# Four value blocks in the lead, and the outputs of a recurrence group made behind its chain

## The chip, the cores and the metric

The kernel runs on one core of one Trainium2 chip. The metric is the device time of one execution in microseconds (us), lower is better. Of several executions the median is compared; one more execution was profiled, and all views come from that one.

## The reference, cut to what matters

A trunk of two layers over 256 tokens and 2048 channels, in float32. Layer 0 mixes tokens with an RWKV-7 recurrence, layer 1 with differential attention; each is followed by a gated MLP. Only layer 0's mixer is touched:

```python
def rwkv7_mix(x, v_first, vres, mu, w_rkv, ...):
    xx = token_shift(x) - x                       # x of the token before, less x
    xr, xw, xk, xv, xa, xg = (x + xx * mu[i] for i in range(6))
    r, k, v = xr @ w_rkv[0], xk @ w_rkv[1], xv @ w_rkv[2]
    w = -softplus(-(w0 + tanh(xw @ w1) @ w2)) - 0.5          # low-rank: decay
    a = sigmoid(a0 + (xa @ a1) @ a2)                         # low-rank
    g = sigmoid(xg @ g1) @ g2                                # low-rank
    ...
    # 32 heads of 64: S_t = S_{t-1} (diag(w_t) + a_t^T b_t) + v_t^T k_t ;  y_t = S_t r_t
    y = wkv7_scan(r_h, decay, k_h, v_h, -kk, kk * a_h)
    ...
    return (group_norm(y) + bonus) * g @ w_o
```

## The kernel before

Everything is kept transposed: a tile holds 128 channels (one *block*) by 256 tokens, and there are 16 blocks of the 2048 channels (`KT`). Products in full float32 precision are made of three faster ones: `split` and `chunk` cut a number into a rounded part `hi` (a ScalarE cast) and the rest `lo` (a subtraction on VectorE, `L219` for weights and `L197` for inputs), and hi*hi, hi*lo and lo*hi are summed in PSUM. An input tile holds its hi and lo parts side by side, 512 columns. `mm3` makes the three products either as one of 512 columns and one of 256 (`L231`, `L232`) or, when `narrow`, as three of 256 in one half bank (`L227`, `L228`, `L229`). Weights come from memory in chunks of four k-blocks (256 KB, `L210`), into the pools `raw`, `hi` and `lo`, whose buffer counts `PACE["vw"]` sets for this stage.

The work is written as Python generators; each `yield` ends a step, and `_together` interleaves several generators by the share of their steps. A scheduler of the framework then orders each engine's queue, and may move an instruction past others of its engine. Queues run in order.

Layer 0 has these stages. In the *lead*, `lead` feeds `mix(3, ...)`, which loads the input blocks (`L775`), makes `xx` and the mixed input of the value product into the tile `S0`, and beside it runs the products of the first value blocks (`lg` of them), going through the k-blocks in step with the input. For the first `ramp` k-blocks the products of the two blocks alternate (`L251` to `L255`). Then `_together` runs the rest of the value products in pairs (`dense_pair`) beside `loras`, which mixes three more inputs into the tile `S1` (the chip's rows say `S1r`) and makes the three low-rank products. Then the r and k products of the first group follow, beside the mix for k.

Then comes the recurrence, in eight groups of two blocks (four heads). `pipeline` runs at once the `chain` and `outputs` of a group, the `lanes` of the next one, the `front` of the one behind it and the r and k products of the one behind that. `lanes` inverts 64x64 triangles in small products (`L1254` to `L1302`). `chain` goes through the four chunks of 64 tokens: it finishes R (`L1369`), copies it, makes U (`L1381`) and copies it, and makes the next state S (`L1392`, `L1396`). The outputs y of a chunk (PSUM tile `yps`) are two kinds of products: of the state (`L1373`), written just behind `L1369`, and of U and V (`L1402`), written just behind `L1392`. `outputs` normalizes y of the group. Single PSUM tiles `us`, `b0`, `b1`, `yps` serve all groups.

Of the kernel before, what the change touches and what calls it, by code (L numbers as in the profile page):

```python
# [36 lines left out]
            4), lb=1, early=46.23, vw=(8, 5, 5), vp=2, ep='V', eg='A', lg=2, lr=2, la=4, ah=10, ao=12, ah0=0.05)  # L37
# [92 lines left out]
class Trunk:  # L130
# [103 lines left out]
    def dense_steps(self, src, n, xs, evac, group=1, k0=0, step=4, pool=False, narrow=False,  # L234
                    ramp=0):

        for g in range(0, len(src), group):
# [4 lines left out]
            while done < n:  # L242
                if done < ramp:

                    chunks = [(ps[j], *next(its[j])) for j in js]
                    s = chunks[0][2]
                    for i in range(s):
                        x = xs[:, k0 + done + i, :]
                        w = slice(i * P, (i + 1) * P)
                        for p, _, _, hi, lo in chunks:  # L250
                            self.nc.tensor.matmul(p[:, :T], lhsT=hi[:, w], rhs=x[:, :T], start=done + i == 0,  # L251
                                                  stop=False)
                            self.nc.tensor.matmul(p[:, T:], lhsT=lo[:, w], rhs=x[:, :T], start=False, stop=False)
                        for p, _, _, hi, lo in chunks:
                            self.nc.tensor.matmul(p[:, T:], lhsT=hi[:, w], rhs=x[:, T:], start=False, stop=False)  # L255
                        yield
                    done += s
                    continue
# [248 lines left out]
    def lead(self, feed, group, *args, ramp=0, ahead=4):  # L507
# [246 lines left out]
    def rwkv(self, ahead=None):  # L754
        nc, tc = self.nc, self.tc
        with ExitStack() as ctx:
# [5 lines left out]
            with ExitStack() as c1:  # L762
                gr = Groups(self, c1, S1, V, mids)
                with ExitStack() as c2:
# [6 lines left out]
                    xx = xp.tile([P, KT, T], F32, name="xx")  # L771
                    nc.gpsimd.memset(x[:, :, 0:1], 0.0)
# [6 lines left out]
                    def mix(i, dst, first=False):  # L779
                        for j in range(KT):  # L780
                            if first and j in starts:
                                load(j, starts.get(j))
# [723 lines left out]
```

## Time and profile before

| | |
|---|---|
| median of three runs | 2523.8 us (2520.84 to 2527.0) |
| the profiled execution | 2523.33 us |
| its span in the trace | 2521.6 us |
| TensorE busy (PE) | 2457.5 us, 97% |
| VectorE busy (DVE) | 2012.7 us, 80% |
| ScalarE busy (ACT) | 1640.7 us, 65% |
| GpSimd busy (POOL) | 165.7 us, 7% |
| DMA | 428.70 MB, mean 170 GB/s |
| mean granted TensorE clock | 0.991 |

The profile names engines PE (TensorE's products), PEld (its weight loads), DVE, ACT, POOL and SP (the queue that issues the DMAs). A row of a timeline has the start, the duration, engine, line, operation, output<-input, shape and count, and in brackets the idle time before it with what ended it. A row of the waits has who waited for whom, the sum, the times, and the longest. A row of a group has the count, busy time, mean duration in ns, and the idle time before. By time, the lead lasts until 33.8 us, the stage with it until 154 us, the recurrence until about 617 us.

### The profile page before, as it was taken

How to read it: one execution, taken by the hardware profiler on the slowest of the kernel's cores; microseconds unless marked ns; L12 is line 12 of the kernel's file. 1: busy time of each engine (PE TensorE's matmuls, PEld its weight loads, DVE VectorE, ACT ScalarE, POOL GpSimd, SP SyncE). 2: the span in 40 equal slices, each digit the busy share in tenths (PEclk: the TensorE clock that was granted, in tenths of full speed). 3: DMA queues.
4: the chain of work that ended last, by engine and by line, in shares of the span. 5: the costliest groups of instructions: out<-in, count | busy, mean ns of one | idle time of the engine just before them, and what ended most of it. 6: DMA issues, size and time to landing. Idle time of an engine off the chain costs nothing.

```text
span 2521.6 us, 56316 instructions
## 1 busy us (share of the span) xinstructions
PE 2457.5 (97%) x18626; PEld 2166.4 (86%) x18626; DVE 2012.7 (80%) x5097; ACT 1640.7 (65%) x4237; POOL 165.7 (7%) x232
## 2 busy tenths in 40 slices
PE   7999999999999999999999999999999999999997
PEld 6997888777888888888889899988988888888886
DVE  8978888878997777776776877779987777777776
ACT  5756666545676666665666766666776666666665
POOL 1000000000300000000110200003300000000111
PEclk9999999999999999999999999999999999999998
DMA  6644443344465555666766555556465555566664
GB/s 211 199 127 108 111 107 103 106 126 126 142 200 189 190 190 190 189 190 198 215 188 188 151 167 175 169 178 184 152 200 188 188 187 189 187 188 187 189 189 139
DMA packets 276742, 428.70 MB, mean 170 GB/s; under 512 B 60632, under 2 KB 83168, under 8 KB 276448
## 3 DMA queue, kind: packets, MB, share of 16 engines
q1 hardware_dynamic: 276448, 425.10, 55.7%
q8 instruction: 146, 2.39, 0.4%
q14 instruction: 148, 1.21, 0.2%
HBM read 420.25 MB, written 6.31 MB: 169 GB/s over the span
## 4 chain that ended last, share of the span: by engine, by line
PE 81%; DVE 4%; ACT 1%; issue 1%; DMA 1%; POOL 0%; ACTq 0%; DVEq 0%; POOLq 0%
PE psd L231 43%; PE psd L232 22%; PE psd L227 2%; PE psd L228 2%; PE psd L229 2%; DVE lo L219 1%; PE psd L298 1%; PE psd L299 1%; PE psd L297 1%; DMA raw<-in_ff_up 1%; PE pss L1168 1%; PE lnst L353 0%; DVE S L197 0%; ACT hi L216 0%; PE pss L675 0%
## 5 line engine op out<-in xcount | busy, mean ns | idle before, releaser
L216 ACT CAST hi<-raw 128x256 fp32r<-128x256 f32 (+1 forms) x3036 | 1219.2, 410 | 690.5 <-PE psd L231 464.5
L219 DVE TENSOR_TENSOR lo<-raw,hi 128x256 fp32r<-128x256 f32 (+1 forms) x3034 | 1303.0, 439 | 417.2 <-ACT hi L216 373.4
L231 PE MATMUL psd<-S,hi 128*128 128x512 f32 x3000 | 1054.5, 395 | 2.6 <-DVE S L197 1.4
L232 PE MATMUL psd<-S,lo 128*128 128x256 f32 x3000 | 841.1, 280 | 3.0 <-DVE lo L219 3.0
L231 PEld LDWEIGHTS psd<-S,hi 128*128 128x128 f32 x3000 | 565.0, 188 | 133.8 <-ACT hi L216 1.7
L232 PEld LDWEIGHTS psd<-S,lo 128*128 128x128 f32 x3000 | 564.6, 188 | 5.0 <-DVE lo L219 4.7
L231 PE MATMUL psd<-hs,hi 128*128 128x512 f32 x1290 | 451.2, 394 | 0.0
L232 PE MATMUL psd<-hs,lo 128*128 128x256 f32 x1290 | 361.5, 280 | 0.0
L231 PEld LDWEIGHTS psd<-hs,hi 128*128 128x128 f32 x1290 | 241.8, 187 | 56.2 <-ACT hi L216 0.6
L232 PEld LDWEIGHTS psd<-hs,lo 128*128 128x128 f32 x1290 | 243.1, 188 | 0.3 <-DVE lo L219 0.2
L227 PE MATMUL psd<-S,hi 128*128 128x256 f32 x480 | 138.9, 289 | 2.2 <-ACT hi L216 1.9
L229 PE MATMUL psd<-S,lo 128*128 128x256 f32 x480 | 138.6, 289 | 0.7 <-DVE lo L219 0.7
L228 PE MATMUL psd<-S,hi 128*128 128x256 f32 x480 | 137.9, 287 | 0.0
L231 PE MATMUL psd<-S1r,hi 128*128 128x512 f32 x276 | 108.9, 425 | 2.3 <-ACT hi L216 1.1
L227 PEld LDWEIGHTS psd<-S,hi 128*128 128x128 f32 x480 | 90.8, 189 | 6.7 <-ACT hi L216 2.6
L229 PEld LDWEIGHTS psd<-S,lo 128*128 128x128 f32 x480 | 90.7, 189 | 5.7 <-issue 3.0
L228 PEld LDWEIGHTS psd<-S,hi 128*128 128x128 f32 x480 | 91.0, 190 | 2.0 <-issue 1.7
L227 PE MATMUL psd<-S1r,hi 128*128 128x256 f32 x284 | 85.7, 302 | 0.1
L231 PE MATMUL psd<-S1a,hi 128*128 128x512 f32 x240 | 84.6, 396 | 0.0
L371 POOL COPY ln_acc<-X 128x256 f32<-128x256 f32 x4 | 2.0, 511 | 1242.6 <-DVE X L405 1242.6
L232 PE MATMUL psd<-S1r,lo 128*128 128x256 f32 x276 | 82.0, 297 | 1.4 <-DVE lo L219 1.4
L546 DVE SCALAR_TENSOR_TENSOR gc<-gp,cpar,gc 128x256 f32<-128x256 f32 x172 | 82.2, 478 | 0.0
(304 smaller groups left out, 3541.6 us busy)
## 6 DMA issues: line engine op xcount, KB each, us to landing
raw<-in_ff_up SPq DMA_DIRECT2D x676, 256.0 KB, 3.4
raw<-in_ff_down SPq DMA_DIRECT2D x320, 256.0 KB, 2.9
raw<-in_rkv SPq DMA_DIRECT2D x192, 256.0 KB, 3.7
raw<-in_da_qk SPq DMA_DIRECT2D x122, 256.0 KB, 3.4
raw<-in_da_v SPq DMA_DIRECT2D x64, 256.0 KB, 3.0
raw<-in_da_o SPq DMA_DIRECT2D x64, 256.0 KB, 3.7
raw<-in_rw_o SPq DMA_DIRECT2D x50, 256.0 KB, 3.4
raw<-in_ff_down SPq DMA_DIRECT2D x32, 192.0 KB, 2.6
```

The source lines that it names most:

```text
L216: nc.scalar.copy(out=hi[:, :s * P], in_=r)
L219: eng.tensor_tensor(out=lo[:, :s * P], in0=r, in1=hi[:, :s * P].bitcast(F32), op=ALU.subtract)
L227: nc.tensor.matmul(ps[:, :T], lhsT=hi, rhs=xs[:, :T], start=first, stop=False)
L228: nc.tensor.matmul(ps[:, :T], lhsT=hi, rhs=xs[:, T:], start=False, stop=False)
L229: nc.tensor.matmul(ps[:, :T], lhsT=lo, rhs=xs[:, :T], start=False, stop=last)
L231: nc.tensor.matmul(ps, lhsT=hi, rhs=xs, start=first, stop=False)
L232: nc.tensor.matmul(ps[:, T:], lhsT=lo, rhs=xs[:, :T], start=False, stop=last)
L297: nc.tensor.matmul(o, lhsT=xh, rhs=hi, start=k == 0 and b == 0, stop=False)
L298: nc.tensor.matmul(o, lhsT=xh, rhs=lo, start=False, stop=False)
L299: nc.tensor.matmul(o, lhsT=xl, rhs=hi, start=False, stop=k == KT - 1 and b == T // P - 1)
L546: nc.vector.scalar_tensor_tensor(out=gc, in0=g[:, k:k + T], scalar=cw(k, j), in1=gc, op0=ALU.mult, op1=ALU.add)
L1168: nc.tensor.matmul(ps[:, n * P:(n + 1) * P], lhsT=KB[hr, uu, :, :], rhs=AR[hr, uu, :, :], start=True, stop=True)
```

## The change

Two edits. In the lead, four value blocks instead of two go through the k-blocks with the input, each with its own PSUM bank and in narrow form; there is no `ramp`, and the lo parts of the lead's first chunks are made on VectorE, not on GpSimd. The mixed input of the lead is made without `xx`, as (1 - mu) x_t, scaled on ScalarE (`L777`), plus mu x_(t-1) on VectorE (`L778`). `xx` is made later, in four operations of 1024 columns on VectorE, ahead of the first low-rank mix; in all later mixes two blocks are split at once, 512 columns wide. The pools hold 9 raw, 8 hi and 8 lo chunks instead of 8, 5 and 5, and PSUM has six banks here instead of four. The four value blocks are evacuated by one ScalarE copy each.

In the recurrence, all y products of a group are written behind its fourth chunk, for which all states of the group are kept (six state tiles instead of two). `chain` and `lanes` have one more step each.

```diff
-            4), lb=1, early=46.23, vw=(8, 5, 5), vp=2, ep='V', eg='A', lg=2, lr=2, la=4, ah=10, ao=12, ah0=0.05)
+            4), lb=1, early=46.23, vw=(9, 8, 8), vp=4, ep='V', eg='A', lg=4, la=4, ah=10, ao=12, ah0=0.05)
@@ dense_steps
-                if done < ramp:
...
 def lead
-                steps = self.dense_steps(*args, group=group, pool=True, ramp=ramp)
+                steps = self.dense_steps(*args, group=group, narrow=True)
@@ rwkv
-                    def mix(i, dst, first=False):
-                        for j in range(KT):
...
-                                eng = nc.vector if j in (0, 4, 8, 12) else nc.gpsimd
-                                eng.tensor_tensor(out=xx[:, j, :], in0=x[:, j, 0:T], in1=x[:, j, 1:],
-                                                  op=ALU.subtract)
...
+                    def mix(i, dst, first=False, diff=False):
+                        for j in range(0, KT, 1 if first else 2):
...
+                                nc.scalar.activation(out=t, in_=x[:, j, 1:], func=AF.Copy, scale=om[:, j:j + 1])
+                                nc.vector.scalar_tensor_tensor(out=m, in0=x[:, j, 0:T], scalar=self.p(f"mu{i}", j),
+                                                               in1=t, op0=ALU.mult, op1=ALU.add)
+                                self.split(m, dst[:, j, :])
...
+                            if diff and j % 4 == 0:
+                                self.tc.keep_in_program_order(
+                                    nc.vector.tensor_tensor(out=xx[:, j:j + 4, :], in0=x[:, j:j + 4, 0:T],
+                                                            in1=x[:, j:j + 4, 1:], op=ALU.subtract))
...
+                            self.split(m, dst[:, j:j + 2, :])
...
-                    evv = lambda j, ps: self.total(ps, V[:, j, :])
+                    evv = lambda j, ps: nc.scalar.copy(out=V[:, j, :], in_=ps[:, :T])
...
-                                       for j in range(n, KT, 2))), 13 * 5))
+                                       for j in range(n, KT, 2))), 11 * 5))
@@ Groups.open
-        self.Ss = [fx.tile([P, GT, C], F32, name=f"S{i}") for i in range(2)]
+        self.Ss = [fx.tile([P, GT, C], F32, name=f"S{i}") for i in range(2 * (NC - 1))]
@@ lanes
         nc.vector.tensor_copy(out=Z2[rows[3]], in_=pv[rows[3]])
         yield
+        yield
@@ chain
-                for jj in range(GT):
-                    for h in range(2):
-                        nc.tensor.matmul(yps[rows[h], jj, cs], lhsT=S[rows[h], jj, :],
-                                         rhs=AR[rows[h], jj * NC + c, 1, :], start=jj == 0, stop=False)
...
+            S = Sn
+            yield
+
+        for c in range(NC):
+            cs = slice(c * C, (c + 1) * C)
+            if c:
+                for jj in range(GT):
+                    for h in range(2):
+                        nc.tensor.matmul(yps[rows[h], jj, cs], lhsT=states[c - 1][rows[h], jj, :],
+                                         rhs=AR[rows[h], jj * NC + c, 1, :], start=jj == 0, stop=False)
             for jj in range(GT):
                 for h in range(2):
                     nc.tensor.matmul(yps[rows[h], jj, cs], lhsT=UV[:, jj, c, h, :], rhs=m(jj, h, c)[:, C:],
                                      start=c == 0 and jj == 0, stop=jj == GT - 1)
-            S = Sn
-            yield
+        yield
```

What the scheduler makes of it, at three places. A row is one instruction, or several equal ones that follow each other. First VectorE's queue in the middle of the lead, before: `mx` is the mixed input, `xz` the input, `S_76` the tile `S0`.

```order
L792 SCALAR_TENSOR_TENSOR mx<-xx,par,xz 128x256 x3
L197 TENSOR_TENSOR S_76<-mx,S_76 128x256 x2
L792 SCALAR_TENSOR_TENSOR mx<-xx,par,xz 128x256
L197 TENSOR_TENSOR S_76<-mx,S_76 128x256
L219 TENSOR_TENSOR lo<-raw,hi 128x512
L197 TENSOR_TENSOR S_76<-mx,S_76 128x256
L789 TENSOR_TENSOR xx<-xz 128x256
L219 TENSOR_TENSOR lo<-raw,hi 128x512
```

And the same queue in the changed kernel (`mp` is the mixed input now):

```order
L778 SCALAR_TENSOR_TENSOR mp<-xz,par,mp 128x256
L219 TENSOR_TENSOR lo<-raw,hi 128x512
L778 SCALAR_TENSOR_TENSOR mp<-xz,par,mp 128x256
L197 TENSOR_TENSOR S_76<-mp,S_76 128x256
L219 TENSOR_TENSOR lo<-raw,hi 128x512
L197 TENSOR_TENSOR S_76<-mp,S_76 128x256
```

In the lead one lo part of weights now stands between any two input blocks; sixteen are in it instead of six, and the differences `xx` have gone behind it.

Second, TensorE in group 3 around R of chunk 1, before (`S_2191` is the state behind chunk 0, `psd` rows are dense products of another group):

```order
L1392 MATMUL us<-UV,KBT 64x64 x4
L1402 MATMUL yps<-M,UV 64x64 x4
L1227 MATMUL pss<-cst,KB 128x128 x4
L227 MATMUL psd<-S_76,hi 128x256
L1369 MATMUL b_5972<-S_2191,AR 64x64
L1369 MATMUL b_5973<-S_2191,AR 64x64
L1369 MATMUL b_5972<-S_2191,AR 64x64
L1369 MATMUL b_5973<-S_2191,AR 64x64
L1373 MATMUL yps<-AR,S_2191 64x64 x4
L228 MATMUL psd<-S_76,hi 128x256
```

After it ten more dense products come, and then `L1381`, which needs R. In the changed kernel (`L1389` is the old `L1392`, `L1377` the old `L1381`, `L1409` and `L1405` the two kinds of y products):

```order
L1389 MATMUL us<-UV,KBT 64x64 x4
L1227 MATMUL pss<-cst,KB 128x128 x4
L227 MATMUL psd<-S_76,hi 128x256
L228 MATMUL psd<-S_76,hi 128x256
L1409 MATMUL yps<-M,UV 64x64
L1369 MATMUL b_5884<-S_2101,AR 64x64
L1369 MATMUL b_5885<-S_2101,AR 64x64
L1369 MATMUL b_5884<-S_2101,AR 64x64
L1369 MATMUL b_5885<-S_2101,AR 64x64
L1409 MATMUL yps<-M,UV 64x64 x3
L1405 MATMUL yps<-AR,S_2101 64x64 x3
L1377 MATMUL us<-R,M 64x64 x4
```

The y products were written behind the whole chain, but the scheduler has drawn some of them forward into the chain as soon as their inputs exist. Between the state products and the use of R only six of them are left. Of the 28 of such a group, ten stand in one run behind the last U.

Third, ScalarE in the same group, where the copy of the lanes' last intermediate (`L1295`) stands; before:

```order
L1075 COPY M<-W_5075 32x8x32 x2
L844 CAST l_5872<-l2r 128x256
L1320 ACT_TABLE_LOAD
L1320 ACTIVATE wa<-psd,par 128x256
L1295 COPY T_5828<-pss 32x256
L1320 ACTIVATE wa<-psd,par 128x256
L1075 COPY UV<-us 64x2x2x128 x2
```

and in the changed kernel:

```order
L309 ACTIVATE o_rs<-Lx 128x512
L1295 COPY T_5740<-pss 32x256
L844 CAST l_5761<-l2r 128x256
L1075 COPY M<-W_4987 32x8x32
L1321 ACT_TABLE_LOAD
L1321 ACTIVATE wa<-psd,par 128x256
L1309 COPY M<-pss 32x8x32
L1321 ACTIVATE wa<-psd,par 128x256
L1075 COPY UV<-us 64x2x2x128
```

The copy has moved ahead of the table load, with the additional step of the lanes; the second copy of `UV` has moved behind the sigmoids.

More of the change, by code (lines that the diff above doesn't have):

```diff
@@ L232, in mm3, with dense_steps @@
             nc.tensor.matmul(ps[:, T:], lhsT=lo, rhs=xs[:, :T], start=False, stop=last)
-    def dense_steps(self, src, n, xs, evac, group=1, k0=0, step=4, pool=False, narrow=False,
-                    ramp=0):
+    def dense_steps(self, src, n, xs, evac, group=1, k0=0, step=4, pool=False, narrow=False):
         for g in range(0, len(src), group):
@@ L242, in dense_steps @@
             while done < n:
-                if done < ramp:
[L245 to L255, printed above, removed]
-                        yield
-                    done += s
-                    continue
                 for j in js:
@@ L505, in ln_finish, with lead @@
             nc.sync.dma_start(out=out[:, j:j + 2, :], in_=xs)
-    def lead(self, feed, group, *args, ramp=0, ahead=4):
+    def lead(self, feed, group, *args, ahead=4):
         fed = 0
@@ L777, in rwkv @@
                     starts = {0: 1, 1: 2, 2: 4, 4: 6, 6: 8, 8: 10, 10: 12, 12: 14, 14: 16}
[L779 to L794 removed]
+                    def mix(i, dst, first=False, diff=False):
+                        for j in range(0, KT, 1 if first else 2):
+                            if first:
+                                if j in starts:
+                                    load(j, starts.get(j))
+                                if j == 0:
+                                    nc.sync.dma_start(out=self.par[:, :6 * KT], in_=self.a["par"][:, :6 * KT])
+                                    nc.scalar.activation(out=om, in_=self.p(f"mu{i}", 0, KT), func=AF.Copy, scale=-1.0,
+                                                         bias=1.0)
+                                if j == 8:
+                                    self.load_consts()
+                                m = xt.tile([P, 2, T], F32, name="mp")
+                                t, m = m[:, 0], m[:, 1]
+                                nc.scalar.activation(out=t, in_=x[:, j, 1:], func=AF.Copy, scale=om[:, j:j + 1])
[3 more added lines that the diff above has]
+                                yield
+                                continue
+                            if diff and j % 4 == 0:
+                                self.tc.keep_in_program_order(
+                                    nc.vector.tensor_tensor(out=xx[:, j:j + 4, :], in0=x[:, j:j + 4, 0:T],
+                                                            in1=x[:, j:j + 4, 1:], op=ALU.subtract))
+                            m = xt.tile([P, 2, T], F32, name="mp")
+                            for k in range(2):
+                                nc.vector.scalar_tensor_tensor(out=m[:, k], in0=xx[:, j + k, :],
+                                                               scalar=self.p(f"mu{i}", j + k), in1=x[:, j + k, 1:],
+                                                               op0=ALU.mult, op1=ALU.add)
+                                if k == 0:
+                                    yield
+                            self.split(m, dst[:, j:j + 2, :])
@@ L798, in loras @@
                         for i, mi, fn in ((0, 1, AF.Tanh), (1, 4, None), (2, 5, AF.Sigmoid)):
-                            yield from mix(mi, S1)
+                            yield from mix(mi, S1, diff=i == 0)
                             def ev(_, ps, i=i, fn=fn):
@@ L814, in rwkv @@
                     self.lead(mix(3, self.S0, True), n, [rkv[2][j] for j in range(n)], KT, self.S0, evv,
-                              ramp=PACE["lr"], ahead=PACE["la"])
+                              ahead=PACE["la"])
                     _together((loras(), 4 * 16 + 3 * 5),
```

18 lines of the change are left out of this document (6 added, 12 removed).

## The prediction

> **What bounds the kernel now.** I read the page's engine shares first, then who TensorE waits for in the first stage, then the busy time by stage.
>
> ```profile
> span 2521.6 us, 56316 instructions
> PE 2457.5 (97%) x18626; PEld 2166.4 (86%) x18626; DVE 2012.7 (80%) x5097; ACT 1640.7 (65%) x4237; POOL 165.7 (7%) x232
> PE psd L251 <- ACT hi L216: 8.8, 2, 8.0
> PE psd L232 <- DVE lo L219: 2.5, 1, 2.5
> 8.00:26.50 18.50, 11.47 (x37) 8.90 (x38) 16.18 (x31) 8.63 (x22) 9.59 (x11) 0.82 0.65 224
> 33.80:154.00 120.20, 119.50 (x959) 116.72 (x958) 112.04 (x253) 82.40 (x175) 3.94 (x15) 1.00 0.59 182
> 277.00:469.00 192.00, 186.41 (x3029) 160.43 (x3028) 167.71 (x437) 125.08 (x301) 2.78 (x12) 1.00 0.40 106
> ```
>
> TensorE is busy 97% of the span, so time is won only where it stands still, runs at half clock, or repeats work. The two waits are the longest of the first 33.8 us; in the stage rows the columns after the length are TensorE, weight loads, VectorE, ScalarE, GpSimd, then granted clock, DMA share and GB/s. From 33.8 to 154 TensorE has no hole, but VectorE is nearly as full (112 of 120). The profiled run took 2523.3 us, 1.7 more than its span, and 0.5 below the median 2523.8; the sum is made against 2523.3. Everything behind layer 0's recurrences stands in the same order before and after, so only the first 617 us count.
>
> **The lead: TensorE's side.**
>
> ```profile
> 7.36 0.62 ACT L216 CAST hi<-raw 128x512 fp32r<-128x512 f32 x1 [2.95 <-DMA raw<-in_rkv]
> 22.98 0.58 PE L232 MATMUL psd<-S,lo 128*128 128x256 f32 x1 [2.45 <-DVE lo L219]
> 24.00 0.63 PE L231 MATMUL psd<-S,hi 128*128 128x512 f32 x1
> 24.64 0.63 PE L231 MATMUL psd<-S,hi 128*128 128x512 f32 x1
> 26.95 0.39 PE L231 MATMUL psd<-S,hi 128*128 128x512 f32 x1
> 27.30 0.39 PE L231 MATMUL psd<-S,hi 128*128 128x512 f32 x1
> 33.83 0.28 PE L229 MATMUL psd<-S,lo 128*128 128x256 f32 x1
> 154.14 0.29 PE L227 MATMUL psd<-mid,l 128*128 128x256 f32 x1
> ```
>
> A 512- and a 256-column product take 0.64 us at 24.0 (half clock) and 0.35 at 26.95 (full): 0.213 or 0.117 us per 256 columns. The three narrow products of the new code are the same 768 columns, so the change of form costs nothing. Two blocks are 2 x 16 x 3 x 0.117 = 11.2 us of work, yet their last product is issued just before 33.83: about 22 us are lost. The first cast ends at 8.0 and waited for its transfer; the new queue has the same transfers ahead of that one, so 8.0 stays. The first lo part, now on VectorE, is ready 0.7 later, at 8.7. One step (a chunk of four k for one block) is 12 narrow products: 2.56 us at half clock. VectorE and ScalarE supply one in about 1.4 us (below), so TensorE has no more holes, and its clock should open as it did before: 4.0 us after the dense run that starts at 22.98 the spacing is short. So 19 products run until 12.7, and the other 173 take 20.2: the lead ends near 33.0, with four blocks instead of two. The rest of the stage, to 154.14, shrinks by the 0.8 us and by 96 products (11.3): TensorE alone would end it at 142.0, a gain of 12.1.
>
> **The lead: VectorE's side.**
>
> ```profile
> L792 DVE SCALAR_TENSOR_TENSOR mx<-xx,par,xz 128x256 f32<-128x256 f32 x6 | 5.3, 940 | 0.0
> L197 DVE TENSOR_TENSOR S<-mx,S 128x256 fp32r<-128x256 f32 x5 | 3.5, 745 | 0.0
> L219 DVE TENSOR_TENSOR lo<-raw,hi 128x512 fp32r<-128x512 f32 x44 | 29.4, 679 | 0.0
> L792 DVE SCALAR_TENSOR_TENSOR mx<-xx,par,xz 128x256 f32<-128x256 f32 x44 | 19.6, 473 | 0.0
> L197 DVE TENSOR_TENSOR S1r<-mx,S1r 128x256 fp32r<-128x256 f32 x41 | 15.7, 411 | 0.1
> L216 ACT CAST hi<-raw 128x512 fp32r<-128x512 f32 x42 | 26.1, 620 | 10.8 <-PE psd L228 4.9 <-ACT hi L216 2.3 <-PE psd L231 2.1
> L196 ACT CAST S1r<-mx 128x256 fp32r<-128x256 f32 x41 | 16.1, 407 | 5.7 <-DVE mx L792 5.5
> 24.13 1.26 DVE L792 SCALAR_TENSOR_TENSOR mx<-xx,par,xz 128x256 f32<-128x256 f32 x3
> 26.31 1.10 DVE L197 TENSOR_TENSOR S<-mx,S 128x256 fp32r<-128x256 f32 x3 [0.92 <-ACT S L196]
> 29.03 1.89 DVE L219 TENSOR_TENSOR lo<-raw,hi 128x512 fp32r<-128x512 f32 x3
> 30.00:142.00 112.00, 111.30 (x879) 108.05 (x879) 110.30 (x253) 83.34 (x181) 0.00 (x0) 1.00 0.63 195
> ```
>
> The first two rows are of 9 to 18 us, the next five of 40 to 100. While GpSimd made differences and lo parts beside it, VectorE's multiply-add took 940 ns instead of 473 and its split 745 instead of 411. The change takes all fourteen GpSimd operations of the lead away, so I count the quiet durations; were the slow ones to stay, 29 such operations would cost about 12 us more, which I exclude because nothing is left on GpSimd there. Back to back they overlap: three in a row take 1.26, 1.10 and 1.89, so each beyond the first adds 0.39, 0.345 and 0.60 us.
>
> From the first lo part (8.0) the lead needs 16 lo (9.6), 12 multiply-adds (4.7) and 13 splits (4.5): 18.8 us, to 26.8. ScalarE's share is as long: 12 steps of a cast (0.62), an input cast and the new scaled copy (no row shows it; I take 0.41 like the input cast, as the operand is as wide), 1.37 with overlap, and 4 casts, 18.9. They hand to each other, so I add 1.2 for such stalls: 28.0. Bounds: 26.8, and 32 if each of 12 steps lost 0.4.
>
> Behind it VectorE must make, until the last lo of the first r products, 68 lo (48 value, 12 low-rank, 8 r; 40.8 us), 80 multiply-adds (31.2), 40 splits now two blocks wide (24.0 at the lo's 0.60, the same 512 columns), 4 differences of 1024 columns (no row; stretching 411 and 679 gives 1.22, less overlap 1.15; 4.6) and 9 small ones (3.1): 103.7, to 131.7. The totals of the whole stage hardly change: the wide splits save 40 x (0.69 - 0.60) = 3.6 and the two evacuations 0.7, the differences and the two lo parts that GpSimd had cost 5.8. TensorE would want that last lo at 129.2 (142.0 less 11.4 for the k products and 1.4 for one chunk). VectorE is 2.5 late; with 0.5 of latency TensorE is held to 145.0. The old code had 110.3 of 112 us here, so the stage was as much VectorE's as TensorE's, and deeper weight buffers (8 instead of 5) create no capacity. I take another 1.1 for short waits on the way: 146.1, **a gain of 8.0 us**. The ends are 12.1 (no lag) and 4 (VectorE at 32).
>
> The transfers: 16 chunks (4.2 MB), the inputs (2.1), parameters and constants (0.3), 6.6 MB, go ahead of the last step.
>
> ```profile
> 0.00:10.00 10.00, 1.21 (x4) 0.92 (x4) 1.95 (x5) 2.92 (x4) 3.98 (x10) 1.00 0.72 206
> 10.00:20.00 10.00, 6.22 (x24) 4.92 (x23) 10.00 (x16) 3.90 (x10) 7.72 (x10) 0.99 0.84 296
> ```
>
> With 2.1 MB in the first 10 us (206 GB/s) and 296 GB/s from then on they are in at 25.2, and the last step's cast and lo part end at 26.5, beside VectorE's 26.8: the cover is there, but thin; a quarter slower behind 10 us would cost 5, which the end of 32 holds. The four evacuations become one ScalarE copy each, behind casts, with six banks free: nothing.
>
> **The recurrence.** The number of y products is the same. Their order is not one run: in groups 1 to 4 it is cut into pieces.
>
> ```profile
> PE pss L1302 <- ACT T L1295: 0.8, 1, 0.8
> PE pss L1263 <- DVE M L1171: 0.3, 1, 0.3
> PE pss L1123 <- DVE bon L1191: 0.3, 1, 0.3
> 374.06 1.28 ACT L1320 ACT_TABLE_LOAD   x1
> 375.85 0.36 ACT L1295 COPY T<-pss 32x256 f32<-32x256 f32 x1
> 371.03 0.28 PE L228 MATMUL psd<-S1r,hi 128*128 128x256 f32 x1
> 371.15 0.28 PE L229 MATMUL psd<-S1r,lo 128*128 128x256 f32 x1
> 371.36 0.73 PE L1282 MATMUL pss<-W,Z 32*32 32x16 f32 x64
> PE us L1392 <- DVE UV L1075: 0.8, 1, 0.8
> PE b L1369 <- DVE S L1396: 0.8, 1, 0.8
> 229.01 0.69 PE L1293 MATMUL pss<-T,M 32*32 32x32 f32 x32 [0.98 <-DVE T L1287]
> 230.00:240.00 10.00, 9.37 (x66) 6.87 (x65) 6.71 (x20) 6.85 (x16) 0.00 (x0) 0.66 0.15 36
> ```
>
> The three waits are all of group 2 (325 to 373 us). For: the copy L1295 now stands ahead of the table load on ScalarE, so the 0.8 goes, in five groups 4. There are 14 fewer runs of small products in all; entering one costs 0.09 (0.21 against 0.12 in the rows of 371) and leaving it 0.03, so 1.7. Against: between the state product and the use of R stood 11 narrow products, now six tiny ones; both copies of R need a semaphore and about 0.2 us, so 0.3 once per group. L1168 comes ahead of VectorE's last AR operation (about 0.6), L1263 loses four products of cover (0.5), and L1123 waits for a VectorE chain that is no shorter. That is 1.4 in four groups, 5.6. Net 0.1; I take **-0.5**. Ends: 6 of gain; and 6 of loss, if each of eight groups takes the 0.8 us of a bare hand-over, as the rows at L1392 and L1369 show it in the last groups. The extra step in the lanes queues nothing new; the order shows what waits behind it.
>
> The sum: 2523.3 - 8.0 - 0.5 = 2514.8, said as 2515.
>
> **Rivals.** (a) VectorE, late in the lead, eats most of the gain: 32 instead of 28 leaves 4, and the chain gives back 1: 2520. For it: 110.3 of 112; against: GpSimd no longer slows it. (b) All goes well: no VectorE lag (12.1), the chain's 6 and no half clock: 2505 or less. (c) Slower, through the clock in the recurrence. In the row at 230 the granted clock is 0.66, just after a wait of 1.0 us amid tiny products: 6.8 of the 10 us ran at half clock, which costs 3.4. If the new waits (1.4 per group) do the same, with 1.0 for themselves beyond what goes, it is 4.4 in each of six groups, 26, less the lead's 8, and the time is 2541; from 2.2 us per group on it is measurably slower. Against: group 2 has 1.3 us of waits and a granted clock of 1.00. [...] (d) The lead's clock stays half: 192 x 0.213 puts its end at 49.6 instead of 33.0, past the 45.1 where it breaks even, and the time at 2528; only holes would do that, and supply is faster than TensorE's 2.56.
>
> **Numbers.** Forecast 55% (2509 to 2519), (a) 22%, (b) 14%, (c) 6%, (d) 3%. The range goes from (b)'s edge into (a) and a little beyond: 2505 to 2524. A measurement tells 0.2%, 5 us, from no change: faster 0.72 (forecast and (b), with a little of (a)), same 0.21, slower 0.07.
>
> **What would show it.** Right: the fourth block's last lead product near 33, the half clock gone by 13 to 16 us, VectorE without 0.9-us multiply-adds, TensorE waiting for lo (L219) between 40 and 130 us by some 3 us in all, and the low-rank products that follow the k products near 146. L1303 without its 0.8; small new waits at L1377, L1168 and L1263. Wrong: a wait for hi or a transfer inside the lead, VectorE done with it later than 30, or half-clock windows in groups 1 to 4.

## The result, and the profile after

The changed kernel takes 2511.57 us (median of four runs, 2508.72 to 2513.36) beside 2523.57 for the kernel before in the same session: a ratio of 0.9948, 95% interval 0.9934 to 0.9963, or 12 us less. The same kernel, timed again on another occasion (below), gave 2511.32 and a ratio of 0.9959 (0.9946 to 0.9971). The forecast was 2515, within 2505 to 2524. The profiled execution took 2512.88 us, 10.4 less than the one of before. First two lines of the page, then the busy time by stage, where the columns after the length are TensorE, weight loads, VectorE, ScalarE, GpSimd, clock, DMA share and GB/s.

```profile
span 2510.9 us, 56277 instructions
PE 2461.2 (98%) x18650; PEld 2170.1 (86%) x18650; DVE 2009.3 (80%) x5057; ACT 1635.2 (65%) x4215; POOL 154.5 (6%) x218
```

```profile
13.00:33.00 20.00, 20.00 (x171) 20.00 (x171) 20.00 (x43) 18.19 (x44) 0.00 (x0) 1.00 0.94 312
33.00:145.80 112.80, 109.20 (x867) 105.87 (x866) 105.60 (x204) 70.73 (x129) 4.64 (x15) 1.00 0.57 175
268.70:459.70 191.00, 190.88 (x3027) 164.07 (x3026) 168.07 (x434) 122.28 (x302) 1.88 (x12) 1.00 0.41 106
459.70:629.20 169.50, 160.97 (x1862) 123.61 (x1861) 135.66 (x365) 90.67 (x234) 6.94 (x13) 0.98 0.41 119
```

From 13 to 33 us TensorE and VectorE have no hole now and GpSimd does nothing; behind it TensorE stands still for 3.6 of 112.8 us. In the four steady groups (268.7 to 459.7) TensorE is busy 190.9 of 191.0 us, where it was busy 186.4 of 192.0: nearly all waits are gone, and yet the stretch is hardly shorter. The row of before for the last groups and the way to the next stage:

```profile
468.70:638.20 169.50, 158.41 (x1863) 123.28 (x1862) 136.01 (x364) 90.78 (x233) 6.97 (x13) 0.96 0.41 119
```

It has the same 169.5 us, though a granted clock of 0.96 there stands for 13.7 us at half clock, and the 0.98 after for 6.8. Next, rows of TensorE's and VectorE's timelines of the changed kernel at the edges of the lead: the first product, three where the spacing changes, the fourth block's last lead product, VectorE's last two lo parts of the lead with the first difference, and the first low-rank product behind the k products.

```profile
7.61 0.58 PE L227 MATMUL psd<-S,hi 128*128 128x256 f32 x1 [7.61 <-ACT hi L216]
12.90 0.37 PE L228 MATMUL psd<-S,hi 128*128 128x256 f32 x1
13.11 0.28 PE L229 MATMUL psd<-S,lo 128*128 128x256 f32 x1
13.23 0.28 PE L227 MATMUL psd<-S,hi 128*128 128x256 f32 x1
26.50 1.30 DVE L219 TENSOR_TENSOR lo<-raw,hi 128x512 fp32r<-128x512 f32 x2
27.71 1.23 DVE L785 TENSOR_TENSOR xx<-xz 128x1024 f32<-128x1024 f32 x1
32.90 0.28 PE L229 MATMUL psd<-S,lo 128*128 128x256 f32 x1
145.79 0.29 PE L227 MATMUL psd<-mid,l 128*128 128x256 f32 x1
```

The spacing from issue to issue falls from 0.21 to 0.12 us at 13.1: there the half clock ends. It is read from the spacing, since the clock records of this execution begin only at 13.1, with 1.00. The lead ends at 32.90 with four blocks, and the stage at 145.79 instead of 154.14. So the account of the two profiled executions, by the starts of the same products:

| stretch | before | after | difference |
|---|---|---|---|
| to the first low-rank product behind the k products | 154.14 | 145.79 | -8.35 |
| from there to where the order is the same again, behind the recurrence | 484.04 | 483.44 | -0.60 |
| of this, groups 1 to 4 | 191.71 | 190.96 | -0.75 |
| from there to the last product | 1867.37 | 1865.68 | -1.69 |

The last row has the same instructions in the same order, so I put it down to the executions and not to the change. No single event makes it: before waits 1.4 us for a cast at 1411 and then has 3.4 us at half clock, which cost 1.7, but later waits of after take most of that back, and 1.3 is left by 1423 us; after has 3.4 us at half clock of its own at 637.7, and smaller shifts of both signs make the rest. The -0.60 is not clean either. The clock records show 20.5 us at half clock in the recurrence of before and 10.2 in that of after, worth up to 5.1 us; whether the new order or the execution made this difference, two traces cannot tell. Groups 1 to 4 have no half clock in either, so the -0.75 is the order's own.

### The profile page after: what moved, and what is told of

It reads as the page before. It is cut to its first block, busy times and chain, and to the rows that moved or that the text cites. A ratio compares the mean times of both kernels' runs of the same rounds, so it can differ in the third digit from the quotient of the medians.

```text
span 2510.9 us, 56277 instructions
## 1 busy us (share of the span) xinstructions
PE 2461.2 (98%) x18650; PEld 2170.1 (86%) x18650; DVE 2009.3 (80%) x5057; ACT 1635.2 (65%) x4215; POOL 154.5 (6%) x218
## 4 chain that ended last, share of the span: by engine, by line
PE 90%; DVE 5%; DMA 2%; ACT 1%; issue 1%; SPq 0%; POOL 0%; ACTq 0%; DVEq 0%; POOLq 0%
PE psd L231 44%; PE psd L232 22%; PE psd L227 4%; PE psd L229 4%; PE psd L228 4%; DVE lo L219 2%; PE psd L281 1%; PE psd L280 1%; PE psd L282 1%; PE pss L1168 1%; PE psd L916 1%; DMA raw<-in_rkv 1%; PE psd L917 1%; PE psd L915 1%; DMA raw<-in_rw_o 1%
## 5 line engine op out<-in xcount | busy, mean ns | idle before, releaser
L231 PE MATMUL psd<-S,hi 128*128 128x512 f32 x2976 | 1043.8, 395 | 0.0
L231 PEld LDWEIGHTS psd<-S,hi 128*128 128x128 f32 x2976 | 559.6, 188 | 129.3
L227 PE MATMUL psd<-S,hi 128*128 128x256 f32 x512 | 148.8, 291 | 9.5 <-ACT hi L216 9.2
L229 PE MATMUL psd<-S,lo 128*128 128x256 f32 x512 | 149.2, 291 | 3.7 <-DVE lo L219 3.7
L228 PE MATMUL psd<-S,hi 128*128 128x256 f32 x512 | 146.8, 287 | 0.0
L227 PEld LDWEIGHTS psd<-S,hi 128*128 128x128 f32 x512 | 97.8, 191 | 13.2 <-ACT hi L216 9.6
L229 PEld LDWEIGHTS psd<-S,lo 128*128 128x128 f32 x512 | 97.6, 191 | 9.9 <-DVE lo L219 7.0
L228 PEld LDWEIGHTS psd<-S,hi 128*128 128x128 f32 x512 | 98.0, 191 | 1.2 <-issue 1.2
L232 PE MATMUL psd<-S1r,lo 128*128 128x256 f32 x276 | 82.7, 300 | 0.3 <-DVE lo L219 0.3
L229 PE MATMUL psd<-S1r,lo 128*128 128x256 f32 x284 | 80.7, 285 | 0.3 <-DVE lo L219 0.2
## 6 DMA issues: line engine op xcount, KB each, us to landing
raw<-in_ff_down SPq DMA_DIRECT2D x32, 192.0 KB, 2.6
```

Source lines behind the costliest of these rows:

```text
L227: nc.tensor.matmul(ps[:, :T], lhsT=hi, rhs=xs[:, :T], start=first, stop=False)
L228: nc.tensor.matmul(ps[:, :T], lhsT=hi, rhs=xs[:, T:], start=False, stop=False)
L229: nc.tensor.matmul(ps[:, :T], lhsT=lo, rhs=xs[:, :T], start=False, stop=last)
L231: nc.tensor.matmul(ps, lhsT=hi, rhs=xs, start=first, stop=False)
L232: nc.tensor.matmul(ps[:, T:], lhsT=lo, rhs=xs[:, :T], start=False, stop=last)
```

## The experiments

All are compared with the kernel before in the same session, where that took 2521.7 to 2522.5 us.

**The two edits apart.** First the new lead with the old recurrence:

```diff
-        self.Ss = [fx.tile([P, GT, C], F32, name=f"S{i}") for i in range(2 * (NC - 1))]
+        self.Ss = [fx.tile([P, GT, C], F32, name=f"S{i}") for i in range(2)]
...
         nc.vector.tensor_copy(out=Z2[rows[3]], in_=pv[rows[3]])
         yield
-        yield
...
+                        nc.tensor.matmul(yps[rows[h], jj, cs], lhsT=S[rows[h], jj, :],
+                                         rhs=AR[rows[h], jj * NC + c, 1, :], start=jj == 0, stop=False)
...
-                        nc.tensor.matmul(yps[rows[h], jj, cs], lhsT=states[c - 1][rows[h], jj, :],
-                                         rhs=AR[rows[h], jj * NC + c, 1, :], start=jj == 0, stop=False)
```

The products of U and V go back behind each chunk's U likewise.

> The changed kernel with the recurrence of the kernel before (y products behind each chunk, two state tiles, one step less in the lanes); only the lead is new. Theory: the lead is worth 8.1 us, as the start of the first recurrence group shows (146.7 instead of 154.9), and the recurrence edit about 0.9 by the starts behind it; the time is 2514 to 2516, with steady groups of 47.9 us and L1302's 0.8 back. Rival: the lead carries the whole 12 us, and the time is that of the changed kernel, 2511.6.

It took 2513.95 us (2508.06 to 2516.17), ratio 0.9962 (0.995 to 0.9975). The stage ends at 145.46, the steady groups take 47.92 us, and their waits are back (waits of TensorE in the four of them):

```profile
PE pss L1302 <- ACT T L1295: 3.2, 4, 0.9
```

Second, the kernel before with the recurrence edit alone (the same hunks the other way round).

> The kernel before with the recurrence edit alone. Theory: 1.4 us of waits go in each of four steady groups, but 14 more changes from one kind of small product to another (0.12 each) less 4 fewer visits from dense products take 1.2 of it back: steady groups of 47.7 instead of 47.9, 2522 to 2523.5 in all. Rival: the edit is worth some 3 to 4 us in all, 2520.

2521.09 us, ratio 0.9998 (0.9989 to 1.0007); three of the four steady groups take 47.69, one 48.15. So the lead carries the gain, and the recurrence edit is worth nothing that could be measured.

**The changed kernel again**, without an edit.

> The changed kernel once more, beside the next ones on the same chip. The account of the traces gives 8.3 us for the lead and about 1 for the recurrence, 2512 to 2515 beside a kernel before of 2522 to 2524; if the gain is 12 and more, something behind the recurrence or in other executions adds to it.

2511.32 us (2510.43 to 2513.19), the stage at 145.73 and steady groups of 47.68: as before. The ratio makes the gain 10.3 us (7.3 to 13.6), and the 9 us of the account lie within that. The inside of the stage differs, though: the first product comes at 8.60 instead of 7.61, the full clock at 14.6, and the lead ends at 34.01 instead of 32.90, but TensorE then waits less for lo (from 0 to 150 us):

```profile
PE psd L229 <- DVE lo L219: 2.2, 4, 1.1
```

So an end of the lead 1.1 later left the end of the stage where it was.

**The y products in one run.** The next two ask where the steady groups lost what their waits gave back. One pins the 28 y products behind each other:

```diff
+        keep = t.tc.keep_in_program_order
...
-                        nc.tensor.matmul(yps[rows[h], jj, cs], lhsT=states[c - 1][rows[h], jj, :],
-                                         rhs=AR[rows[h], jj * NC + c, 1, :], start=jj == 0, stop=False)
+                        keep(nc.tensor.matmul(yps[rows[h], jj, cs], lhsT=states[c - 1][rows[h], jj, :],
+                                              rhs=AR[rows[h], jj * NC + c, 1, :], start=jj == 0, stop=False))
```

The products of U and V are pinned likewise.

> The changed kernel with the y products of a group pinned behind each other, so that all 28 stand in one run. Theory of the hand-overs: in a steady group 4 changes of kind and one visit fewer, at 0.12 each 0.6 us, so steady groups of 47.1 and 2508 to 2509.5 in all, with no new wait. Rival: the price of a change of kind is not real (the 1.2 us went into something else), and the groups stay at 47.7. Second rival: the run stands late and the group's outputs wait for it, with a wait of TensorE at L1429 or at the next group's first products of 0.5 or more.

The other pins them too, but writes the twelve of the states ahead of the sixteen of U and V:

```diff
-        for c in range(NC):
-            cs = slice(c * C, (c + 1) * C)
-            if c:
-                for jj in range(GT):
+        for c in range(1, NC):
+            for jj in range(GT):
...
+        for c in range(NC):
+            for jj in range(GT):
```

> As e3_y_run, but first the twelve y products of the states and then the sixteen of U and V, so that the kind changes once within the run instead of seven times. Theory of the hand-overs: 5 more changes go, another 0.6 us per steady group: 46.5, and 2505 to 2507 in all. Rival: a change of kind costs nothing in itself, and the two kernels take the same time. If only changes of the rows of the array count (both kinds alternate between them in the same way), the groups differ by less than 0.2.

They took 2520.14 us (2513.59 to 2524.06) and 2517.51 (2510.76 to 2521.05), ratios 0.9986 (0.9976 to 0.9997) and 0.9976 (0.9965 to 0.9987): the first gives most of the gain away, the second about half of it. In the traces the steady groups take 48.4 to 49.3 and 47.6 to 50.1 us (the 50.1 with 3.4 us at half clock in it). First the run itself, in one kernel and in the other (a kind of product, its start, and the first product behind the run; counts are of records, two to a product):

```profile
349.93 0.45 PE L1410 MATMUL yps<-M,UV 128*64 128x64 f32 x8
350.31 0.45 PE L1406 MATMUL yps<-AR,S 64*64 64x64 f32 x8
...
352.59 0.60 PE L1168 MATMUL pss<-AR,KB 64*128 64x128 f32 x6
```

```profile
350.97 0.92 PE L1404 MATMUL yps<-AR,S 64*64 64x64 f32 x24
351.82 1.15 PE L1409 MATMUL yps<-M,UV 128*64 128x64 f32 x32
352.90 0.49 PE L1168 MATMUL pss<-AR,KB 64*128 64x128 f32 x4
```

From its first product to the L1168 behind it the run takes 2.66 us with six changes of kind inside, and 1.93 with one, in all four groups alike: 0.73 for five, 0.15 each. The price of a change of kind is real. What was not foreseen is the other side. The two largest waits of TensorE in the four steady groups of the first of the two, and one place of its timeline:

```profile
PE psd L227 <- ACT hi L216: 3.3, 4, 1.4
PE us L1377 <- ACT R L1075: 1.8, 4, 0.5
```

```profile
330.53 0.34 PE L1369 MATMUL b<-S,AR 64*64 64x64 f32 x8
331.33 0.27 PE L1377 MATMUL us<-R,M 64*64 64x64 f32 x2 [0.46 <-ACT R L1075]
```

Without y products between L1369 and L1377, the copy of R lies bare (0.46), and dense products wait for weights (0.8 once a group on average). The wait of the second rival, for the group's outputs, came in one group of the four (0.6). The pieces that the scheduler drew forward were cover. The same place in the changed kernel has no wait:

```profile
331.19 0.34 PE L1369 MATMUL b<-S,AR 64*64 64x64 f32 x8
331.47 0.45 PE L1409 MATMUL yps<-M,UV 128*64 128x64 f32 x6
331.84 0.38 PE L1405 MATMUL yps<-AR,S 64*64 64x64 f32 x5
332.01 0.27 PE L1377 MATMUL us<-R,M 64*64 64x64 f32 x1
```

The profiled execution of the first pinned kernel lies 6.5 us below its median; what its other runs lost beyond these waits no trace shows.

**The useful part of the recurrence edit alone.** The new lead, the old recurrence, and one copy moved:

```diff
-        nc.scalar.copy(out=Z2[rows[1]], in_=pv[rows[1]])
+        nc.vector.tensor_copy(out=Z2[rows[1]], in_=pv[rows[1]])
```

> The new lead, the recurrence of the kernel before, and there one copy (L1295) on VectorE instead of ScalarE, so that it does not stand behind a table load. Theory: of what the recurrence edit did in a steady group, only the end of L1302's wait of 0.8 was of use; here it comes without the 14 more changes of kind, so steady groups of 47.1 to 47.4, and the time 2 to 4 us below the kernel with the new lead alone (2511 to 2512 beside 2514). Rival: the copy on VectorE waits there as long behind others (0.5 or more stays at L1302) and the groups keep 47.9.

2509.33 us (2506.84 to 2512.11), ratio 0.9949 (0.9936 to 0.9962). The steady groups disagree with the expectation: 48.4 to 48.6, with other waits in place of L1302's:

```profile
PE yps L1402 <- ACT UV L1075: 3.3, 4, 1.0
PE psd L227 <- ACT wa L1320: 1.5, 4, 0.5
```

The median is lower all the same, but the intervals overlap, both with the new lead alone and with the changed kernel. In the trace the first group takes 118.4 instead of 122.0, and the records show no half clock in it, where those of the changed kernel show 3.4 us (6.8 in its second profile). The kernel with the pinned cast, below, which has the moved copy too, takes 118.5 there with 3.4 us at half clock, and the new lead alone 120.7 with as much. Whether the moved copy did that stays open.

**Why TensorE waits for lo behind the lead.** The prediction had VectorE too late by its total work. In this kernel the mix for the third low-rank input is left out, so that its product takes the second one's input:

```diff
-                            yield from mix(mi, S1, diff=i == 0)
+                            if i < 2:
+                                yield from mix(mi, S1, diff=i == 0)
```

> The changed kernel without the mix for the third low-rank input: its product takes the second one's input. This leaves out sixteen multiply-adds, eight splits and eight casts, 11 us of VectorE work between 33 and 130 us; TensorE's work is unchanged. Theory: VectorE's lateness alone holds TensorE in this stage, so the waits of L229 for lo (3.6 us) go, the first low-rank products behind the k products come at 142 to 142.6 instead of 145.8, and the time falls by 3 to 4. Rival: the waits come from the order of the weights' chunks and not from the amount of work: they stay, and so does 145.8.

2511.27 us. The row of 30 to 142 us, first of the changed kernel, then of this one, and this one's waits of TensorE from 10 to 140:

```profile
30.00:142.00 112.00, 108.40 (x860) 105.07 (x859) 108.60 (x210) 73.02 (x134) 2.96 (x7) 1.00 0.57 177
```

```profile
30.00:142.00 112.00, 108.50 (x858) 104.99 (x858) 98.08 (x186) 68.52 (x126) 3.94 (x15) 1.00 0.59 184
```

```profile
PE psd L229 <- DVE lo L219: 3.5, 5, 1.4
```

VectorE has 10.5 us less to do and TensorE waits as long; the stage ends at 145.91. The theory of the total is refuted. Of the four waits at 42 to 51 us this kernel says nothing, since the mix that it leaves out stands at 77 to 92 us in the changed kernel. The next kernel has two blocks in the lead:

```diff
-  lg=4, ...
+  lg=2, ...
-                                       for j in range(n, KT, 2))), 11 * 5))
+                                       for j in range(n, KT, 2))), 13 * 5))
```

> The changed kernel with two value blocks in the lead instead of four; all else as changed (narrow products, no GpSimd, six banks, deep buffers). Theory: VectorE's total up to the first r products' last lo is the same, and it bounds the stage, so the stage ends only 1.5 to 3 us later, at 147 to 149, and the time is 1 to 3 above the changed kernel. Rival: the two more blocks are what the lead gains, since without them 11 us of TensorE's time in the lead are empty again: the stage ends at 151 to 154 and the time is 5 to 8 above.

2518.55 us (2512.3 to 2522.88), ratio 0.998 (0.9969 to 0.9991), and the stage ends where the rival had it (waits of TensorE from 10 to 140 us, and the first low-rank product behind the k products):

```profile
PE psd L229 <- DVE lo L219: 4.3, 4, 1.6
PE psd L227 <- ACT hi L216: 1.6, 1, 1.6
```

```profile
152.50 0.29 PE L227 MATMUL psd<-mid,l 128*128 128x256 f32 x1
```

Without the two more blocks the 192nd product of the stage's records comes at 40.1 instead of 32.9, and the stage ends 6.7 us later. Not all of this is the blocks: in this execution the records show 3.4 us at half clock from 49.0 us on, 2 us behind the wait of 1.6 for lo, where the changed kernel has none:

```profile
49.00:52.40 3.40, 3.28 (x10) 2.89 (x11) 3.40 (x7) 0.67 (x2) 0.00 (x0) 0.50 0.59 172
```

They cost up to 1.7. So by the traces the two blocks bring 5.0 to 6.7 of the 8.35 us, and the rest of the lead's edit, which no run takes apart, 1.6 to 3.3; the medians are 7.2 apart.

In the changed kernel all of TensorE's waits from 36 us to the stage's end but one of 0.2 lie at these four places (its timeline, then ScalarE's and VectorE's ahead of the first):

```profile
42.03 0.39 PE L229 MATMUL psd<-S,lo 128*128 128x256 f32 x1 [1.53 <-DVE lo L219]
44.03 0.39 PE L229 MATMUL psd<-S,lo 128*128 128x256 f32 x1 [0.32 <-DVE lo L219]
47.97 0.38 PE L229 MATMUL psd<-S,lo 128*128 128x256 f32 x1 [0.42 <-DVE lo L219]
50.76 0.39 PE L229 MATMUL psd<-S,lo 128*128 128x256 f32 x1 [1.11 <-DVE lo L219]
38.50 1.24 ACT L216 CAST hi<-raw 128x256 fp32r<-128x256 f32 x3 [0.79 <-DMA raw<-in_rkv]
39.64 0.61 ACT L196 CAST S1r<-mp 128x512 fp32r<-128x512 f32 x1
40.29 0.69 DVE L197 TENSOR_TENSOR S1r<-mp,S1r 128x512 fp32r<-128x512 f32 x1 [1.69 <-ACT S1r L196]
```

VectorE, 97% busy in this stage, stood still for 1.69 us at 38.6: its split needs the cast L196, and that stood in ScalarE's queue behind casts that waited for transfers. The lo part behind the split is the one that TensorE misses at 42.03. Three kernels take this apart. In the first the differences go behind the first low-rank mix, which is made as in the lead:

```diff
-                            yield from mix(mi, S1, diff=i == 0)
+                            yield from mix(mi, S1, diff=i == 1, late=i == 0)
...
+                            if late:
...
+                                    nc.scalar.activation(out=m[:, k], in_=x[:, j + k, 1:], func=AF.Copy,
+                                                         scale=om[:, j + k:j + k + 1])
+                                    nc.vector.scalar_tensor_tensor(out=m[:, k], in0=x[:, j + k, 0:T],
+                                                                   scalar=self.p(f"mu{i}", j + k), in1=m[:, k],
+                                                                   op0=ALU.mult, op1=ALU.add)
```

> The changed kernel with the mix for the first low-rank input made as in the lead ((1 - mu) x on ScalarE plus mu times the shifted x on VectorE), so that the four differences of 1024 columns come after it, 20 to 40 us later. TensorE's waits for lo lie at 42 to 51 us, just behind the lead. Theory V: the differences and mixes crowded there make VectorE late; without 4.6 us of them the waits fall from 3.6 to 1 or less, the first low-rank products come at 142.5 to 143.5, the time falls by 2 to 3. Theory S: the first wait (1.5 at 42) begins with casts on ScalarE that wait for a transfer, behind which VectorE's next split waits (1.7); sixteen scaled copies in the same queue do not help there: the waits stay at 3 or more, 145 to 147, and the time is the same within 2 us.

2514.65 us, ratio 0.9967 (0.9955 to 0.9979). The waits are no smaller in sum (4.5 us at L229 between 10 and 140), but those at 42 to 51 us are gone, and five stand between 82 and 95 us, 3.2 in all; the first recurrence group starts at 148.99 instead of 146.74. The four differences now run at 50, 53, 59 and 70 us, so the new waits lie over 10 us behind the last of them, among the multiply-adds and splits of the next input. VectorE's stall at 40 us is gone here as well, so this kernel cannot tell the stall from the differences. That the differences themselves make TensorE wait is not shown, and moving them gains nothing. The second kernel has `vw=(11, 7, 7)` for `(9, 8, 8)`.

> The changed kernel with pools of 11, 7 and 7 chunks instead of 9, 8 and 8; all engines keep their order. Two more transfers of weights can be under way ahead of their casts. Theory S: the transfer that lands at 38.5 was issued late because its raw buffer was free only at 34; with two more it lands earlier, ScalarE no longer waits for it, VectorE's wait of 1.7 at 40 goes, and with it the first of TensorE's waits for lo: 1.5 to 2 us less, first low-rank products at 143.5 to 144.5. Theory V: transfers are not the cause, the waits stay at 3.6, or grow since there are fewer hi and lo buffers.

2511.21 us, the stage at 145.48, the waits still 3.5 in sum. The casts of weights no longer waited for transfers, but the queue had moved another transfer behind the added ones, and its cast took their part (timeline of ScalarE and VectorE):

```profile
39.18 0.41 ACT L844 CAST l<-l2r 128x256 fp32r<-128x256 f32 x1 [2.87 <-DMA l2r<-in_l]
40.14 0.69 DVE L197 TENSOR_TENSOR S1r<-mp,S1r 128x512 fp32r<-128x512 f32 x1 [1.45 <-ACT S1r L196]
```

The third pins that cast, on top of the larger raw pool and of the kernel with the moved copy:

```diff
-        nc.scalar.copy(out=w[:, 0], in_=raw)
+        cast = nc.scalar.copy(out=w[:, 0], in_=raw)
+        if g == 0:
+            self.tc.keep_in_program_order(cast)
```

> The kernel of e6_lead_t with pools of 11, 7 and 7, and the cast of the first low-rank weight (L844, not needed before the recurrence) pinned behind what is written ahead of it, so that it does not stand in ScalarE's queue behind the lead, where it waited 2.9 us for its transfer in e10_raw11. Theory S in its second form: any cast there that waits for a transfer holds VectorE's next split; now none waits long, VectorE's wait of 1.5 to 1.7 at 40 goes, TensorE's wait of 1.5 at 42 falls below 0.5, the first low-rank products come at 143.8 to 144.6 instead of 145.8, and the time is 1 to 2 us below that of e6_lead_t (2509.3). Rival: VectorE is as late without it, and the waits behind 42 us stay at 3 or more: 145.4 to 146, and the time of e6_lead_t.

Its first wait and the end of the stage in TensorE's timeline, and its waits from 10 to 140 us:

```profile
42.63 0.39 PE L229 MATMUL psd<-S,lo 128*128 128x256 f32 x1 [0.31 <-DVE lo L219]
144.70 0.29 PE L227 MATMUL psd<-mid,l 128*128 128x256 f32 x1
```

```profile
PE psd L229 <- DVE lo L219: 2.3, 4, 1.1
```

The first wait falls from 1.37 in the kernel that it builds on to 0.31, the sum from 3.5 to 2.3, and the stage ends 1.1 earlier (the forecast had 1.2 to 2). VectorE's stall at 40 us is gone; 0.41 of one stands at 43, again for a cast behind one that waited for a transfer. The waits alone prove little, since the second profile of the changed kernel had 2.2 with no edit and the same end. But six profiles have this stretch as it is in the changed kernel (its two, the new lead alone, the two with pinned y products, the moved copy): in them VectorE stalls 0.9 to 2.1 us at 40 us and the stage ends at 145.46 to 147.11 (the two pinned ones, which have 3.4 us at half clock there, end last), and both numbers of this kernel lie outside. So ScalarE's queue behind a transfer costs about 1 us there. This rests on one profile: with 2508.03 us (2504.54 to 2509.1) and a ratio of 0.9941 (0.9928 to 0.9953) the kernel has the lowest time of all, but the intervals of the ratio overlap with those of the kernel that it builds on and of the changed kernel. The 1.1 at 50 us is still there; VectorE makes four multiply-adds and a split just ahead of that lo part.

**GpSimd in the lead.** Every second lo part of the lead's weights goes back to GpSimd (`self.pool_every = 2` ahead of the lead, 0 behind it).

> The changed kernel with every second lo part of the lead's weights on GpSimd instead of VectorE (eight of sixteen). Theory of the contention: while GpSimd works, VectorE's multiply-adds take 0.7 to 0.95 us instead of 0.48 and its splits 0.6 to 0.75 instead of 0.42, which costs more than the 4.8 us of lo parts taken from VectorE, and the lead's last lo is ready later than 27.8. Rival: the hands count, VectorE's durations stay, and the last lo is ready by 24 to 26.

One run, 2513.27 us, the stage at 148.39, with 3.4 us at half clock from 47.4 us on, behind a wait of 3.1. Groups of 8 to 33 us in this kernel, with mean ns of one and idle time before:

```profile
L197 DVE TENSOR_TENSOR S<-mp,S 128x256 fp32r<-128x256 f32 x13 | 11.8, 906 | 1.0 <-ACT S L196 0.3
L219 POOL TENSOR_TENSOR lo<-raw,hi 128x512 fp32r<-128x512 f32 x8 | 11.2, 1396 | 18.1 <-ACT hi L216 16.4 <-PE psd L229 1.7
L778 DVE SCALAR_TENSOR_TENSOR mp<-xz,par,mp 128x256 f32<-128x256 f32 x12 | 5.7, 474 | 0.3 <-ACT mp L777 0.3
```

The splits take 906 ns instead of 425 (changed kernel, below): those that begin while a GpSimd lo runs end 0.28 us behind it, as at 12.88 to 14.18 beside 12.45 to 13.90; those that began just ahead of one keep 0.41, as at 12.34 to 12.74. The multiply-adds, none of which began while one ran, keep 474, so this run does not try the theory on them; in the kernel before they did, and took 0.83, as at 14.92 to 15.74 beside a GpSimd difference from 14.68 to 15.46. VectorE's last lo of the lead ends at 28.95 instead of 27.80 though it has eight fewer to make, and GpSimd's at 30.10.

## Why the prediction held, and where its steps did not

**The lead's TensorE side: right.** The lead's end was forecast at 33.0 and came at 32.90; the first product is issued at 7.61 (forecast: first cast done at 8.0, first lo part at 8.7), and the clock opens at 13.1 (12.7), so the later opening costs what the early start gave. That it met to 0.1 us is luck: in the six profiles named above the end lies between 31.8 and 34.0, and the full clock comes 3.4 to 6.0 us behind the first product, where the forecast took 4.0.

**The lead's VectorE side: right to 28.0, wrong behind it.** The last lo part of the lead ends at 27.80. The durations, of 8 to 27 us:

```profile
L219 DVE TENSOR_TENSOR lo<-raw,hi 128x512 fp32r<-128x512 f32 x15 | 10.3, 693 | 0.5 <-ACT hi L216 0.5
L778 DVE SCALAR_TENSOR_TENSOR mp<-xz,par,mp 128x256 f32<-128x256 f32 x12 | 5.8, 485 | 0.7 <-ACT mp L777 0.7
L197 DVE TENSOR_TENSOR S<-mp,S 128x256 fp32r<-128x256 f32 x13 | 5.5, 425 | 0.0
L777 ACT ACTIVATE mp<-xz,om 128x256 f32<-128x256 f32 x12 | 6.1, 505 | 0.9 <-DMA xz<-in_x 0.9
```

The slow durations did vanish with GpSimd's work; the scaled copy takes 0.505, not 0.41, which the slack of ScalarE held; the difference of 1024 columns takes 1.23 (1.22). The sum behind the lead (146.1, a gain of 8.0) met the 145.79 and 8.35 by luck, for the step that set it is refuted: "VectorE is 2.5 late" at the last lo of the r products. At 133 us TensorE waits 0.2 there, and taking 10.5 us of work from VectorE changes nothing. The sum held 4.1 us of lateness (2.5, 0.5 and 1.1); 3.6 were waited, but elsewhere. The 0.5 of latency no run shows: the product at 42.03 starts 0.05 us behind the end of a lo part, and so does the one at 133. These waits, forecast as "some 3 us" between 40 and 130, all lie between 42 and 51 us but for the 0.2. About 1 us of them goes with the stall behind a transfer in ScalarE's queue; the rest comes while VectorE works without a break, and what in its order decides there stays open. A budget of a whole stage said how little slack there was, not where it would break. Nor was it so that VectorE's bound made the number of blocks unimportant: four instead of two are worth 5.0 to 6.7 us.

**The recurrence: -0.5 forecast, -0.6 measured, by terms that were both wrong.** The agreement is luck, the more so as the two executions differ by 10 us at half clock there. L1303's wait went, as forecast, and so did those at L1263 and L1123. The three new waits (1.4 per group, 5.6 in all) did not come: a steady group of the changed kernel has no wait of TensorE. The term that failed is "14 fewer runs of small products", priced at 1.7 of gain. It counted visits from dense products and not changes among small ones. In the four steady groups, by the issue times of the traces, pairs of neighbouring small products with another tile shape rise from 28 to 92, at 0.15 us from issue to issue against 0.02 for two lines of the same shape: 64 x 0.13 = 8.3 us lost. Passages between dense products (`psd`) and small ones of another shape fall from 152 to 112, at 0.09 of extra time to enter and 0.13 to leave, about 0.11: 4.4 won. The net 3.9 of loss takes most of the 5.3 us that the three old waits (0.8, 0.3, and 0.3 in three of the four groups) gave back; of the 1.4 left 0.75 is measured, and the other 0.65 I have not assigned.

**The rivals.** VectorE did not reach the late end (a). Rival (b) came true in its recurrence part only as far as the waits went. For (c), the half clock in the first recurrence group remained, without growing: 3.4 and 6.8 us of it in two profiles of the changed kernel, 6.8 before, none in groups 1 to 4. (d) fell at 13.1 us. The median lies 3.4 us below the forecast. In the profiled executions 1.7 us of the gain lie behind the recurrence, where nothing was changed and which no term of the prediction covers; what makes the rest of the medians' difference no run shows.

## What to carry to other kernels

Where two engines are both full, a stage's sums tell that something will wait, but the wait begins at one place: look for the engine that stands still though it is the full one, and follow the queue that its input stands in. Judge the cure by where the stage ends and not by the sum of the waits, and profile the unedited kernel a second time first: here its waits fell from 3.6 to 2.2 us by themselves, and the end stayed. Among the small products here a change of tile shape took 0.15 us from issue to issue and a change of line in the same shape 0.02, so count the changes among them, not only the visits; but before you gather them in one run, see which waits the scattered pieces cover. More work in a lead that waits for its input is worth what it takes out of the stage behind it, here 5.0 to 6.7 us for two blocks.

## What the runs showed of the hardware

With every second lo part of the lead on GpSimd, VectorE's splits that began while a GpSimd lo part ran ended 0.28 us behind it (1.30 us for 0.42, beside GpSimd's 1.45); one that began 0.11 us ahead kept its 0.41. In the kernel before, a multiply-add that began while a GpSimd difference of 0.79 us ran ended 0.28 us behind it too (0.83 for 0.47). TensorE's clock fell to half for 3.4 or 6.8 us at four places of the recurrence before and at three after; the longest wait of TensorE in the 4 us up to the start of each was 0.8 to 1.3 us. Whether and for how long it did differed from one execution of the same program to the next (3.4 us near 224 in one profile of the changed kernel, 6.8 in the other). Among the dense products behind the lead, 3.4 us at half clock followed the waits of 2.4, 2.7 and 3.1 us (two kernels with pinned y products, GpSimd in the lead) and the one of 1.6 with two blocks, and cost up to 1.7 us beyond the wait each time; in the eight other profiles of the new lead, with waits up to 1.7 in that stage, none did.
